# The low parts of the first projection's weights, and three products of the key blocks, on VectorE in place of GpSimd

## The chip, the cores and the metric

The kernel runs on one core of a Trainium2 chip. The metric is the device time of one execution in microseconds (us); the number to predict is the median of the runs of the changed kernel. The engines are TensorE (PE in the rows, its weight loads PEld), VectorE (DVE), ScalarE (ACT), GpSimd (POOL) and the queues of SyncE (SP), which issue the loads here.

## What is computed

A network of two blocks on 512 tokens of width 1024, all in float32. The first block is a hybrid mixer (a gated delta rule and a state space part, both in two directions) and an expert-choice feed-forward; the second has two layers of feed-forward, three kinds of attention and feed-forward. The change lies in the first mixer alone, whose beginning is

```python
proj = jnp.einsum('bld,dp->blp', n, w_in)                # 1024 -> 6720 columns
conv_in, gates, scal = jnp.split(proj, [CONV_CH, CONV_CH + GATE_CH], axis=-1)
c = jax.nn.silu(centred_dwconv(conv_in, conv_w, conv_b))  # 7 taps along the tokens
q, k, v, xs, Bm, Cm = jnp.split(c, [...], axis=-1)
...
kk = jnp.einsum('bnhid,bnhjd->bnhij', k, k)               # in gated_delta_chunked
A = jnp.where(strict, beta[..., :, None] * kk * decay, 0.0)
sol = lax.linalg.triangular_solve(A, rhs, left_side=True, lower=True, unit_diagonal=True)
```

## The kernel before

**Products in three.** A float32 product is made of three matmuls of a reduced float32 type: a weight tile of 1024 rows by 128 columns is loaded as `raw`, ScalarE copies its rounded high part to `whi` (L225), and another engine subtracts it to get the low part `wlo` (L226, in `weights`, called by `tiles`). `mm3` then runs high weights by high operands (L248), high by low (L249) and low by high (L250), eight times a tile. Each of `raw`, `whi` and `wlo` has two buffers in a ring, and `tiles` asks for a tile's weights one tile ahead. Which engine subtracts is an argument (`eng`); without one it is VectorE, as in the later feed-forwards.

**The projection.** `mix1_in` walks over 53 column tiles in a fixed order (`mix1_tiles`): keys, queries, values, inputs and states go through a convolution, gates do not. Tile i's low part is made by GpSimd up to the seventh tile from the end and by VectorE in the last six (L552). The first two tiles' weights are asked for earlier, while the input is turned, with GpSimd named there too (L2476). What follows a convolved tile: VectorE scales the product out of PSUM into `pad` (L603), ScalarE makes the first tap (L605), VectorE the other six (L609, two operands in SBUF), ScalarE the Silu (L615), and for values and inputs TensorE turns the result by token (L642). A gate is one VectorE operation (L671) and a Silu (L672). `mix_dve` and `step` spread these operations over the following tiles.

**The key blocks.** Once the keys are normed, `gdn_base` multiplies the keys of each chunk with themselves into a bank of PSUM, four heads at a time (L1105). ScalarE copies the bank to `KK` (L1107) and GpSimd takes the diagonal out in place (L1108), eight times. ScalarE copies the diagonal blocks together (L1115), VectorE transposes them (L1117), and for each direction GpSimd multiplies the decays by them (L1138) and VectorE by the step sizes (L1140). `gdn_forward` then does the substitution in 62 VectorE operations (L1154, L1157) between the taps, and four transposes (L1161, L1162).

**Order.** Every engine works through its instructions in a fixed order. A framework puts them in that order when the kernel is built, by places and priorities; an engine waits at the first one whose input is not there. Banks of PSUM: four for tiles' products, three for everything else, one for sums.

Of the kernel before, what the change touches and what calls it, by code (L numbers as in the profile page):

```python
# [25 lines left out]
def host_consts():  # L26
    """Tables that depend on the shapes alone."""
# [83 lines left out]
class Net:  # L111
# [14 lines left out]
    def psum_cfg(self, **bufs):  # L126
        """banks by use"""
        if self.ps_es is not None:
            self.ps_es.close()
        self.ps_es = ExitStack()  # L130
        self.ps = self.ps_es.enter_context(self.tc.tile_pool(name="psum", bufs=2, space=PSUM))
        self.ps_bufs = bufs

    def soon(self, n=300):
        """what frees a bank goes before other work of its engine"""
        return self.tc.high_priority(offset=n)

    def log_exp(self, done=None):
        """the tables with both functions, once the last activation of other ones is out"""
        with self.tc.issue_after(done.ins) if done is not None else ExitStack():  # L140
            self.nc.scalar.preload_act_table_set("natural_log_exp_and_others")
# [15 lines left out]
    def setup_first(self, p):  # L157
        """what the first operands need"""
# [47 lines left out]
    def ring(self, es, raw=2, hi=2, lo=2):  # L206
        """buffers of the weights on their way, for the whole network"""
# [9 lines left out]
    def weights(self, srcs, kt, cols, eng=None):  # L217
        """srcs: [(columns or None, dram ap [128, kt, n])]"""
# [10 lines left out]
    def tiles(self, reqs, eng=None, depth=1, then=None):  # L229
        """weights of each request (arguments of weights()) in turn, loaded ahead; then: requests of what comes next"""  # L230
# [28 lines left out]
    def sq_acc(self, pool, src, acc, first, tag="sq", bufs=2, last=False, scale=1.0, eng=None):  # L259
        """acc (+)= (src * scale)**2, or the last squares on their own"""  # L260
# [11 lines left out]
    def rstd_sum(self, pool, accs, n, tag="rstd", bufs=1, eps=EPS):  # L272
        """sum over partitions and accs / n + eps, by token"""
# [10 lines left out]
    def rstd_row(self, pool, v, tag="rstd", bufs=1):  # L284
        """v ** -0.5 by token, and as a row on every partition"""
# [22 lines left out]
    def rs(self):  # L308
        """inverse norms of the operands' tokens, made when first asked for"""
# [4 lines left out]
    def norm_open(self, side):  # L314
        """scratch of the preparation of the next operands, until norm_done()"""
# [3 lines left out]
    def norm_done(self):  # L319
# [5 lines left out]
        if self.accs2 is not None:  # L325
            # norm of a norm: (v * (w / v + eps)) ** -0.5, and the inner one for the residual
# [5 lines left out]
    def newton(self, pool, r, v, tag="nw"):  # L332
        """r <- r * (1.5 - 0.5 * v * r * r), r near v ** -0.5"""
# [6 lines left out]
    def split(self, hi, lo, src, scale=None, src2=None):  # L340
        """hi + lo == src * scale"""
# [10 lines left out]
class FFN:  # L352
# [9 lines left out]
    def prep(self, k, wv):  # L362
        """split xT[k] * wv into the operand pair and add its squares to the running sum"""
# [12 lines left out]
    def by_token(self, k, wv):  # L376
        """xT[k] * wv with the tokens on the partitions"""
# [11 lines left out]
    def prep2(self, k, w, wv):  # L389
        """prep() for operands that are normed twice, with w in between; the squares come in norm_done()"""  # L390
# [14 lines left out]
    def norm_residual(self, w):  # L405
        """the residual itself, after the first of two norms"""
# [4 lines left out]
    def load_x(self, p, wv=None, between=None):  # L411
        """the input with the features on the partitions, as operand pairs, or as the residual in two kinds of pieces"""
# [30 lines left out]
    def first_norm(self, p):  # L443
        """inverse norms of the input's tokens"""
# [62 lines left out]
# how far the delta rule is emitted before each of the last tiles of the projection  # L507
# [3 lines left out]
class Mix1:  # L511
# [1 line left out]
    def mix1_tiles(self):  # L513
        """column tiles of the projection in the order in which they are taken: (kind, tile)"""
# [21 lines left out]
    def step(self, n=1):  # L536
        """one more piece of everything that is under way"""
# [9 lines left out]
    def mix1_in(self, es_tab, es_qkv, then=None):  # L547
        """es_tab, es_qkv: what outlives the projection until the end of the mixer, of the delta rule"""
# [3 lines left out]
        W = self.tiles(self.mix1_reqs(), eng=lambda i: G if i < len(order) - 6 else V, then=then)  # L552
# [13 lines left out]
        # small weights  # L566
# [14 lines left out]
        # step biases and decay rates, the same on every partition  # L581
# [15 lines left out]
        # ---- what follows each kind of column tile  # L597
# [21 lines left out]
        def heads(n, f, ps):  # L619
            """queries or keys of a head, and their squares' sum by token"""  # L620
            if n == "q":
                # their norms come in with those of the output: see GDN.squares()
# [57 lines left out]
        for i, (n, f) in enumerate(order):  # L680
            n_[0] = i + 1
            if i >= len(order) - len(AHEAD):
                # what is left of the projection needs nothing but the operands: the delta rule begins meanwhile
# [32 lines left out]
    def mix_dve(self):  # L716
        """finish the taps of the oldest column tile, turn about with the next one's and the block inverses"""
# [13 lines left out]
    def sums(self, pn, h, sq):  # L731
        """sum of sq over the partitions, by token, into column h of each chunk"""
# [4 lines left out]
    def head_rows(self, p, pn, n, eps=EPS):  # L737
        """sums of squares of 8 heads by token -> (sum / n + eps) ** -0.5 in stacked rows"""
# [23 lines left out]
    def go(self, g):  # L762
        """under way, at twice the usual pace"""
        self.live.append(g)
        self.fast.append(g)

    def stack(self, pool, rows, n, tag):
        """rows [n, T] fp32 as exact hi (partitions 0..) and lo (partitions 64..) parts"""
# [8 lines left out]
    def bcast(self, ps, st, r, start=True, stop=True):  # L777
        """row r of a stack on every partition"""
        self.nc.tensor.matmul(ps, self.selr[:, r:r + 1].to_broadcast([128, 128]), st, start=start, stop=stop)

    def decays(self, wk, ps, sb):
        """step sizes and cumulated decays, by token and in rows"""
# [25 lines left out]
        # log1p(e) = 2 atanh(e / (2 + e))  # L808
# [24 lines left out]
        # rows: 16-23, 32-47 forward; 24-31, 48-63 backward  # L833
# [15 lines left out]
        # total decay of each chunk on every partition  # L849
# [18 lines left out]
# places in the order of emission: products of the delta rule's rows; start of the first group, and its early decays  # L868
# [5 lines left out]
class SSD:  # L874
    def wout_reqs(self, part):
        """weights of the output projection: of the delta rule's rows (0) or of the state space rows (1)"""
# [3 lines left out]
    def ssd_out(self, yp, wv, wg, before, after, then):  # L880
        """both directions of the state space part, gated and normed; x + mixed @ w_out; yp: pool of the operands"""
# [20 lines left out]
        # dt * decay to the end of the chunk; ln dt - cumulated decay  # L902
# [43 lines left out]
        def weigh(g, s, dd):  # L946
            """what the state takes in"""
# [4 lines left out]
        def inter(g, s, dd):  # L952
            """what the state gives out"""
# [20 lines left out]
        def decay(g, f, hh):  # L974
            """decays of one head in both directions, times the step sizes"""
# [106 lines left out]
# heads whose gate is GpSimd's  # L1082
# [3 lines left out]
class GDN:  # L1086
    def gdn_base(self):
        """products of the keys of a chunk, and the inverses of the 32 x 32 diagonal blocks, one block on each
        partition"""
# [10 lines left out]
        for c in range(4):  # L1100
            s = slice(c * 128, c * 128 + 128)
            for q in range(2):
# [3 lines left out]
                v = KK[:, c, 4 * q:4 * q + 4, :]  # L1106
                S_.copy(v, ps.rearrange("p (h i) -> p h i", h=4))  # L1107
                G.tensor_tensor(v, v, offd.unsqueeze(1).to_broadcast([128, 4, 128]), op=OP.mult)  # L1108
# [10 lines left out]
        for d in range(2):  # L1119
# [18 lines left out]
            G.tensor_tensor(e, e, kk, op=OP.mult)  # L1138
# [5 lines left out]
    def gdn_forward(self, b, Ab):  # L1144
        """forward substitution, an operation at a time"""
# [18 lines left out]
    def gdn_open(self):  # L1164
        """everything to be emitted for the delta rule in order"""
# [24 lines left out]
        def bc(col):  # L1190
            """[128, 4] of one scalar each head -> over the free dimension"""
# [11 lines left out]
        def unit(s, d, q, t):  # L1203
            """four heads of one chunk in one direction: (place in the order, what to emit)"""
# [8 lines left out]
            def rows():  # L1213
                # block inverses on the diagonal, rows of decays
# [42 lines left out]
            # (I + A)^-1 from its diagonal blocks  # L1257
# [30 lines left out]
            # the scan  # L1288
# [1268 lines left out]
```

## Time and profile before

| | us |
|---|---|
| three runs | 3308.85 (median), 3309.02, 3299.69 |
| span of the profiled execution | 3301.7 |
| granted TensorE clock, mean over the span | 0.977 |
| TensorE, VectorE, ScalarE, GpSimd busy | 3130.6, 1924.6, 1360.2, 716.8 |

The profiled execution's own time is not listed beside its span; the span is 7.2 us under the median of the three runs. A matmul's busy time overlaps with that of the next, so the share of TensorE is not what is left to win. The projection ends at about 415 us of the span; what follows is not touched.

### The profile page before, as it was taken

What the parts mean: (1) busy time and instruction counts of PE and PEld (TensorE: products, weight loads), DVE (VectorE), ACT (ScalarE), POOL (GpSimd) and SP (SyncE); (2) the same over time, 40 slices, a digit from 0 to 9 for tenths busy, and PEclk for the clock granted to TensorE, in tenths of its full rate; (3) what the DMA queues carried; (4) which work ended last, traced back from release to release, by engine and by line L of the source; (5) the groups of instructions that cost most, each with busy time, mean ns of one, the idle gap of its engine ahead of it and who ended that gap; (6) DMA issues with size and microseconds to landing.
All of it is one profiled execution on the core that took longest, in us unless ns stands there. A gap on an engine that the chain in (4) does not pass through costs nothing.

```text
span 3301.7 us, 39167 instructions
## 1 busy us (share of the span) xinstructions
PE 3130.6 (95%) x14939; PEld 2465.8 (75%) x14939; DVE 1924.6 (58%) x2762; ACT 1360.2 (41%) x2181; POOL 716.8 (22%) x509
## 2 busy tenths in 40 slices
PE   8988999799799899999999999999999999999998
PEld 6766799656576578888776788888888776688887
DVE  6889845644799874433768444334443577644432
ACT  5533443244677642222547333223232355632222
POOL 3453246441656610001220100010000222010000
PEclk9999999899899999999999999999999999999999
DMA  3322400314589823333230233333333331033332
GB/s 107 89 68 82 128 20 1 115 48 157 193 311 329 285 71 96 96 94 96 62 84 7 76 97 96 98 94 96 96 95 100 89 78 53 14 91 94 96 95 84
DMA packets 482536, 336.95 MB, mean 102 GB/s; under 512 B 36079, under 2 KB 428718, under 8 KB 482350
## 3 DMA queue, kind: packets, MB, share of 16 engines
q1 hardware_dynamic: 482350, 334.46, 33.5%
q8 instruction: 118, 1.93, 0.2%
q14 instruction: 68, 0.56, 0.1%
HBM read 324.45 MB, written 9.96 MB: 101 GB/s over the span
## 4 chain that ended last, share of the span: by engine, by line
PE 65%; DVE 5%; issue 3%; ACT 2%; POOL 2%; DMA 0%; DVEq 0%; POOLq 0%; ACTq 0%; SPq 0%
PE mm L248 17%; PE mm L250 17%; PE mm L249 17%; PE mm L1536 3%; PE pn L2258 2%; PE aux L2244 1%; PE aux L1646 1%; DVE sbe L2377 1%; PE mm L2299 1%; PE aux L278 1%; PE mm L2301 1%; POOL elo L1523 1%; POOL wlo L1523 1%; DVE elo L1523 1%; PE pn L1536 1%
## 5 line engine op out<-in xcount | busy, mean ns | idle before, releaser
L225 ACT CAST whi<-raw 128x1024 fp32r<-128x1024 f32 (+1 forms) x395 | 406.5, 1029 | 1181.3 <-PE mm L249 1045.9
L250 PE MATMUL mm<-xh,wlo 128*128 128x512 f32 (+1 forms) x2136 | 850.0, 398 | 19.1 <-POOL wlo L226 14.7
L248 PE MATMUL mm<-xh,whi 128*128 128x512 f32 (+1 forms) x2136 | 853.4, 400 | 3.7 <-DVE ckv L1849 2.8
L249 PE MATMUL mm<-xl,whi 128*128 128x512 f32 (+1 forms) x2136 | 848.9, 398 | 0.0
L226 DVE TENSOR_TENSOR wlo<-raw,whi 128x1024 fp32r<-128x1024 f32 (+1 forms) x342 | 411.8, 1204 | 297.6 <-ACT whi L225 288.3
L250 PEld LDWEIGHTS mm<-xh,wlo 128*128 128x128 f32 (+1 forms) x2136 | 406.4, 190 | 115.6 <-POOL wlo L226 18.6
L248 PEld LDWEIGHTS mm<-xh,whi 128*128 128x128 f32 (+1 forms) x2136 | 407.1, 191 | 96.3 <-issue 6.1
L249 PEld LDWEIGHTS mm<-xl,whi 128*128 128x128 f32 (+1 forms) x2136 | 406.5, 190 | 89.3
L269 POOL TENSOR_TENSOR acc<-acc,sq 128x512 f32<-128x512 f32 x46 | 77.9, 1694 | 1555.4 <-ACT sq L266 1251.2
L249 PE MATMUL mm<-hl,whi 128*128 128x512 f32 x704 | 274.6, 390 | 0.0
L248 PE MATMUL mm<-hh,whi 128*128 128x512 f32 x704 | 274.0, 389 | 0.0
L250 PE MATMUL mm<-hh,wlo 128*128 128x512 f32 x704 | 273.9, 389 | 0.0
L609 DVE SCALAR_TENSOR_TENSOR cacc<-pad,cw,cacc 128x512 f32<-128x512 f32 x216 | 221.0, 1030 | 13.6 <-ACT cacc L605 10.6
L481 DVE TENSOR_TENSOR u<-mm,rstd 128x512 f32<-128x512 f32 x88 | 60.8, 691 | 279.4 <-PE mm L250 279.4
L226 POOL TENSOR_TENSOR wlo<-raw,whi 128x1024 fp32r<-128x1024 f32 (+2 forms) x53 | 134.6, 2540 | 233.0 <-ACT whi L225 208.5
L477 DVE TENSOR_TENSOR g<-mm,rstd 128x512 f32<-128x512 f32 x88 | 60.8, 691 | 183.4 <-PE mm L250 182.2
L250 PEld LDWEIGHTS mm<-hh,wlo 128*128 128x128 f32 x704 | 132.2, 188 | 27.5
L248 PEld LDWEIGHTS mm<-hh,whi 128*128 128x128 f32 x704 | 132.1, 188 | 27.5
L249 PEld LDWEIGHTS mm<-hl,whi 128*128 128x128 f32 x704 | 132.2, 188 | 27.2
L1523 POOL TENSOR_TENSOR wlo<-eraw,whi 128x320 fp32r<-128x320 f32 x58 | 80.5, 1396 | 53.5 <-ACT whi L1521 46.4
L2204 ACT ACTIVATE Pt<-mm,smst 128x512 f32<-128x512 f32 (+3 forms) x144 | 75.4, 529 | 26.6 <-DVE smst L2203 21.6
L1523 POOL TENSOR_TENSOR elo<-eraw,ehi 128x320 fp32r<-128x320 f32 x57 | 77.5, 1369 | 36.7 <-ACT ehi L1521 29.4
(677 smaller groups left out, 5150.8 us busy)
## 6 DMA issues: line engine op xcount, KB each, us to landing
raw<-in_ffn_w_gate_dram SPq DMA_DIRECT2D x88, 512.0 KB
raw<-in_ffn_w_up_dram SPq DMA_DIRECT2D x88, 512.0 KB
raw<-in_w_in_dram SPq DMA_DIRECT2D x82, 512.0 KB
raw<-in_ffn_w_down_dram SPq DMA_DIRECT2D x64, 512.0 KB
eraw<-in_w_down_dram SPq DMA_DIRECT2D x52, 512.0 KB
eraw<-in_w_gate_dram SPq DMA_DIRECT2D x48, 512.0 KB
eraw<-in_w_up_dram SPq DMA_DIRECT2D x44, 512.0 KB
raw<-in_w_out_dram SPq DMA_DIRECT2D x32, 512.0 KB
```

The costliest lines, as they stand in the source:

```text
L225: nc.scalar.copy(hi, raw)
L226: (eng or nc.vector).tensor_tensor(lo, raw, hi.bitcast(F), op=OP.subtract)
L248: mm(ps, wh, xh, start=start, stop=False)
L249: mm(ps, wh, xl, start=False, stop=False)
L250: mm(ps, wl, xh, start=False, stop=stop)
L269: (eng or nc.gpsimd).tensor_tensor(acc, acc, s, op=OP.add)
L477: nc.vector.tensor_tensor(g, pg, self.rs, op=OP.mult)
L609: V.scalar_tensor_tensor(ac, pad[:, t:t + T], cw[:, i:i + 1], ac, op0=OP.mult, op1=OP.add)
L1523: eng.tensor_tensor(lo[:, c], raw[:, c], hi[:, c].bitcast(F), op=OP.subtract)
L1536: P.matmul(ps, x if n == 2 else x.bitcast(F), w[i][:, cols], start=first and i == 0, stop=last and i == n - 1)
L2204: S_.activation(h.Pt[:, QOFF[qc]:QOFF[qc] + n], ps[:, :n], AF.Exp, bias=st[:, 0, qc:qc + 1], accum_out=st[:, 1, qc:qc + 1])
L2258: P.matmul(po[64 * r:64 * r + 64, kc * 128:], h.v[:, kc], h.PT[:, o:o + 512 - kc * 128], start=start and kc == 0, stop=stop and kc == 3, s ...
```

## The change

Three edits, and the removal of comments and docstrings, which is left out here.

```diff
-        W = self.tiles(self.mix1_reqs(), eng=lambda i: G if i < len(order) - 6 else V, then=then)
+        W = self.tiles(self.mix1_reqs(), then=then)
...
-                v = KK[:, c, 4 * q:4 * q + 4, :]
-                S_.copy(v, ps.rearrange("p (h i) -> p h i", h=4))
-                G.tensor_tensor(v, v, offd.unsqueeze(1).to_broadcast([128, 4, 128]), op=OP.mult)
+                V.tensor_tensor(KK[:, c, 4 * q:4 * q + 4, :], ps.rearrange("p (h i) -> p h i", h=4),
+                                offd.unsqueeze(1).to_broadcast([128, 4, 128]), op=OP.mult)
...
-            G.tensor_tensor(e, e, kk, op=OP.mult)
+            V.tensor_tensor(e, e, kk, op=OP.mult)
```

The low parts of tiles 2 to 46 are made by VectorE. The diagonal of the key products is taken out by one VectorE operation that reads PSUM and writes `KK`, in place of a ScalarE copy and a GpSimd product. The decays' product with the key blocks is VectorE's, twice.

## Rows read from the trace of the kernel before

**Rows 1.** The page: VectorE's busy tenths in 40 slices of 82.5 us.
```profile
DVE  6889845644799874433768444334443577644432
```

**Rows 2.** Windows, five stages of the projection: length, busy us (instructions) by engine, clock, DMA.
```profile
41.25:95.00 53.75, 49.48 (x219) 39.90 (x220) 47.93 (x68) 26.42 (x37) 19.26 (x7) 0.90 0.28 77
95.00:206.00 111.00, 97.32 (x434) 78.44 (x434) 87.70 (x94) 51.40 (x64) 55.91 (x26) 0.92 0.27 78
206.00:309.00 103.00, 86.34 (x351) 67.33 (x349) 102.60 (x135) 31.81 (x43) 35.96 (x13) 0.93 0.27 75
309.00:371.00 62.00, 54.58 (x237) 43.71 (x238) 58.05 (x60) 21.97 (x32) 20.25 (x8) 0.94 0.35 103
371.00:415.00 44.00, 39.55 (x189) 32.56 (x188) 33.96 (x47) 20.84 (x30) 7.88 (x6) 0.92 0.47 140
```

**Rows 3.** VectorE's timeline: start, time from first start to last end, operation.
```profile
308.35 4.85 DVE L609 SCALAR_TENSOR_TENSOR cacc<-pad,cw,cacc 128x512 f32<-128x512 f32 x7
...
321.59 9.32 DVE L609 SCALAR_TENSOR_TENSOR cacc<-pad,cw,cacc 128x512 f32<-128x512 f32 x7
...
382.40 0.68 DVE L603 TENSOR_TENSOR pad<-mm,rstd 128x512 f32<-128x512 f32 x1
383.00 0.74 DVE L609 SCALAR_TENSOR_TENSOR cacc<-pad,cw,cacc 128x512 f32<-128x512 f32 x1
383.66 1.22 DVE L226 TENSOR_TENSOR wlo<-raw,whi 128x1024 fp32r<-128x1024 f32 x1
384.79 3.11 DVE L609 SCALAR_TENSOR_TENSOR cacc<-pad,cw,cacc 128x512 f32<-128x512 f32 x4
```

**Rows 4.** GpSimd's timeline beside those taps; in brackets the idle time before.
```profile
321.35 2.40 POOL L226 TENSOR_TENSOR wlo<-raw,whi 128x1024 fp32r<-128x1024 f32 x1 [4.64 <-ACT whi L225]
326.94 2.64 POOL L226 TENSOR_TENSOR wlo<-raw,whi 128x1024 fp32r<-128x1024 f32 x1 [3.19 <-ACT whi L225]
```

**Rows 5.** Windows of line 609 alone: length, VectorE busy us (instructions), clock, DMA.
```profile
41.25:95.00 53.75, 22.65 (x28) 0.90 0.28 77
95.00:206.00 111.00, 59.24 (x53) 0.92 0.27 78
206.00:309.00 103.00, 56.42 (x54) 0.93 0.27 75
309.00:371.00 62.00, 54.08 (x52) 0.94 0.35 103
371.00:415.00 44.00, 17.92 (x24) 0.92 0.47 140
```

**Rows 6.** VectorE's timeline: one operation beside a GpSimd split, and the next one alone.
```profile
62.13 2.62 DVE L818 SCALAR_TENSOR_TENSOR dt<-dt,e 128x256 f32<-128x256 f32 x1
...
65.34 0.41 DVE L818 SCALAR_TENSOR_TENSOR dt<-dt,e 128x256 f32<-128x256 f32 x1
```

**Rows 7.** Windows of line 226 alone: length, VectorE and GpSimd busy us (instructions), clock, DMA.
```profile
41.25:95.00 53.75, 0.00 (x0) 19.26 (x7) 0.90 0.28 77
95.00:206.00 111.00, 0.00 (x0) 35.66 (x14) 0.92 0.27 78
206.00:309.00 103.00, 0.00 (x0) 35.96 (x13) 0.93 0.27 75
309.00:371.00 62.00, 0.00 (x0) 20.25 (x8) 0.94 0.35 103
```

**Rows 8.** Groups by line, 0 to 420 us: busy us, mean ns, idle before and its releaser.
```profile
L1108 POOL TENSOR_TENSOR KK<-KK,offd 128x512 f32<-128x512 f32 x8 | 11.9, 1514 | 0.0
L1138 POOL TENSOR_TENSOR Ab<-Ab,kk 128x1024 f32<-128x1024 f32 x2 | 5.7, 2859 | 6.5 <-DVE kk L1117 6.5
```

**Rows 9.** Waits of TensorE, 41.25 to 371 us: total us, times, longest.
```profile
PE aux L642 <- ACT vt L615: 14.8, 4, 4.7
PE mm L250 <- POOL wlo L226: 14.7, 8, 4.5
```

**Rows 10.** TensorE's timeline: the wait at the first tile whose low part VectorE makes.
```profile
378.72 0.79 PE L250 MATMUL mm<-xh,wlo 128*128 128x512 f32 x1 [4.45 <-DVE wlo L226]
```

**Rows 11.** Groups by line, 0 to 420 us: an operation of VectorE on 1024 columns.
```profile
L1140 DVE TENSOR_TENSOR Ab<-Ab,bB 128x1024 f32<-128x1024 f32 x2 | 4.6, 2279 | 1.9 <-POOL Ab L1138 1.9
```

## The prediction

> **What bounds the kernel now.** The change touches one stage, so I first read where VectorE is loaded: its slices show 8 and 9 tenths from the second slice to the fifth [rows 1]. That is the input projection, which ends near 415 us (the later slices of 7 to 9 are the experts', which the change leaves alone). The windows of its stages [rows 2] show VectorE busy for 47.93 of 53.75 us, 87.70 of 111, then 102.60 of 103 and 58.05 of 62. From 206 to 371 us VectorE is simply full, and TensorE is paced by it. TensorE's own column there is no measure, as matmul times overlap; the waits are: before 371 us it stood 14.7 us for low parts from GpSimd and 14.8 us for Silu outputs that came late [rows 9]. Those outputs wait for the taps on VectorE. The clock column says the same: TensorE was granted 0.90 to 0.94 of full speed in every stage, because it had idled.
>
> The second question is what VectorE is full of. Two runs of seven taps, same shape, took 4.85 us at 308.35 and 9.32 us at 321.59 [rows 3]. Beside the second stood two splits of GpSimd, at 321.35 and 326.94 [rows 4]; beside the first none. So one split costs VectorE (9.32 - 4.85) / 2 = 2.2 us of standing still, though it runs on another engine. It is no matter of the tap: a 256-column operation takes 2.62 us beside a split and 0.41 alone [rows 6].
>
> **The change part by part.**
>
> *Splits.* 42 of the GpSimd splits between 41 and 371 us (7, 14, 13 and 8 by stage) go to VectorE [rows 7] (the other three moved ones lie before). What VectorE pays for one is seen at the end of the projection, where it makes them already: 383.66 to the next start at 384.79 is 1.13 us [rows 3]. 42 x 1.13 = 47.5 us are added.
>
> *Holds that go.* From 371 to 415 us, with no split on GpSimd, a tap is 17.92 / 24 = 0.747 us [rows 5]. By that, the taps of the four earlier stages are longer by 22.65 - 28 x 0.747 = 1.7, 59.24 - 53 x 0.747 = 19.6, 56.42 - 54 x 0.747 = 16.1 and 54.08 - 52 x 0.747 = 15.2 us, 52.7 in all. Other VectorE operations were held as well; I count ten in the timeline like the one of rows 6, at about 2.1 us each: four in the first stage (8.6), three in the second (6.4), three in the third (5.8). That makes 10.3, 26.0, 21.9 and 15.2, together 73 us. Bounds: 52.7 (taps alone) and 42 x 2.2 = 92 (every split holds something). The Trainium skill, "SBUF — State Buffer", section "Who interferes with whom", would go further than the count: it has a VectorE instruction with two SBUF inputs contend with a GpSimd instruction that reads SBUF, and the later one blocked until the first is done. By it a hold could last a whole split of 2.4 us, and 42 of them 101 us, 28 more than I count; the two splits of rows 4 held less than their length, so the count stands.
>
> *Mask.* Eight VectorE operations from PSUM, 512 columns, are added. The nearest row is the scaling out of PSUM, 382.40 to 383.00, so 0.60 us each [rows 3], 4.8 in all. Eight ScalarE copies go, which cost nothing there as ScalarE is under half busy [rows 2], and 11.9 us of GpSimd [rows 8]. The added wait: the mask waits for the key product, and the next taps and pads stand behind it; and TensorE, which needs a bank of the three, now waits for VectorE where it waited for ScalarE. I take nothing for that wait, since the ScalarE copies stood behind Silus that waited for the same taps; its bound is one wait of the longest kind in rows 9, 4.7 us.
>
> *Block products.* Two operations on 1024 columns, at the split's 1.13 to 1.22 us [rows 3]; the like of line 1140 has a mean of 2.279 only because the first of its two ran beside a GpSimd product [rows 11]. 2 x 1.2 = 2.4 us. Gone are two GpSimd products, mean 2.859 us, and the 6.5 us that GpSimd's queue stood before them for VectorE's transpose [rows 8], with the next low part queued behind: one of the eight waits of rows 9, the longest or next to it.
>
> *Queues.* The weight loads on SyncE's queue wait for a split to free `raw`; they now wait for VectorE's. The split stands behind the scaling of the tile two before it; that scaling waits for its tile's product, and TensorE has a whole tile to run meanwhile. So the new wait costs nothing while VectorE is within a tile of TensorE. What it costs otherwise is seen at 378.72: 4.45 us, when VectorE was behind [rows 10], and the clock of that stage is 0.92, or 0.08 x 44 = 3.5 us of full-speed work lost [rows 2].
>
> *Sum.* VectorE by stage: 41 to 95 us: -10.3 + 7.9 = -2.4. 95 to 206: -26.0 + 15.8 + 4.8 + 2.4 = -3.0. 206 to 309: -21.9 + 14.7 = -7.2. 309 to 371: -15.2 + 9.0 = -6.2. In time:
> - 41 to 95: VectorE is nearly full, TensorE waits in a chain on it: -3 (0 to -7, the latter with its clock loss of 0.10 x 53.75 = 5.4 back as well).
> - 95 to 206: not full, so its own 3.0 plus the wait behind the block product, 4, plus half of the clock loss of 0.08 x 111 = 8.9: -11 (+3, if the mask holds TensorE up, to -18).
> - 206 to 309: full throughout, so VectorE's sum is the time: -7 (-2, with the low bound of holds, to -13).
> - 309 to 371: by the sum -6; by the parts, a tile is 0.60 + 6 x 0.66 + 1.13 = 5.7 us on VectorE [rows 3], 8 tiles 46, which is -16 with TensorE no slower. I take -10, between them.
> - 371 to 415: the 4.45 us wait comes from VectorE's backlog; half of it goes: -2 (0 to -7).
>
> Together -33 us; the ends, which won't all meet, are about -5 and -60. What follows 415 us is the same instructions, started earlier; nothing in it is timed from the start, so I carry the gain through whole. The span is 3301.7; with the same 7.2 us around it the forecast is 3308.85 - 33 = 3276 us.
>
> **The rivals.**
> 1. *TensorE becomes the bound* and its waits on VectorE go: the two rows of waits, 29.5 us [rows 9], and of the clock loss of the first four stages, 5.4 + 8.9 + 0.07 x 103 + 0.06 x 62 = 25 us [rows 2], some 20, as the rest falls into the waits: -50, 3259. For it: a tile of 5.7 us on VectorE, by parts. Against it: the substitution's operations keep 206 to 309 us full.
> 2. *Only the full stages gain*, -7 - 6 = -13, 3296, because the chains of 41 to 206 us (decays, key norms, key blocks) have their own length. The 14.8 us for Silus speak for it.
> 3. *Given back*: the mask and the chain take back what the full stages gain, 3309, within what can be told apart.
> 4. *Lockstep, slower.* Low parts now come from the engine that is full, and TensorE loses the lead that GpSimd's splits let it have. The mechanism has been seen once, at 378.72 [rows 10]; with the clock that is 4.45 + 3.5 = 8 us a time. If it strikes where VectorE has more work than TensorE, every other one of the 13 tiles from 206 to 309 us and two at the key blocks, eight times in all, it is 64 - 33 = +31, 3340. It decides from about four such waits beyond those that go. Against it: one tile of lead remains, and where VectorE is the bound a TensorE wait costs nothing of its own.
> 5. *The split was rightly GpSimd's.* If the long taps have another cause than the splits, no hold goes, and 47.5 + 4.8 + 2.4 = 55 us are added to a full engine: 3364. The two runs of taps and the pair of equal operations speak against it [rows 3, 4, 6]. The Trainium skill, "Perfetto Trace Analysis", section "Optimizing Scalar/DVE Operations", has a rule on this side: offloading from a saturated VectorE, even to GpSimd, may make sense; it adds that the port they share may defeat it, which is what the trace shows here, at 2.2 us a split.
>
> **How the numbers follow.** Forecast 0.50, rival 1 0.13, rival 2 0.15, rival 3 0.09, rival 4 0.09, rival 5 0.04. A difference under 0.3% (10 us) can't be told from none here. Faster holds the forecast and rivals 1 and 2, 0.78; same 0.09; slower 0.13. The range takes the forecast with most of its bounds and rivals 1 and 2, and stops short of the slower ones: 3250 to 3302.
>
> **What would show it.** Right: no tap over 0.8 us from 41 to 371 us but beside the two affine selects that stay on GpSimd; line 226 on VectorE at 1.22 us, about 51 times by 415 us; the windows of 206 to 371 us shorter, by some 17 us together; the wait of line 250 for low parts, now from VectorE, under 14.7 us; the granted clock of these stages above 0.94. Wrong: taps still at 2.8 us (rival 5); many waits of 4 us of line 250 for VectorE and a lower clock (rival 4); key products waiting for `KK` on VectorE by more than 5 us (rival 3).

## The result, and where the time went

| | before | after |
|---|---|---|
| median of the runs shown, us | 3304.8 (3299.7 to 3309.0) | 3257.5 (3256.5 to 3260.9) |
| span of the profiled execution, us | 3301.7 | 3254.8 |
| mean granted clock of TensorE | 0.977 | 0.982 |

The changed kernel takes 0.9861 of the time, with a 95% interval of 0.9847 to 0.9875: 47 us less, where 33 were forecast. The direction and the range held; the size was short by 14 us.

VectorE's busy tenths, which answer to [rows 1], first: the fuller slices now end at the fourth, and the projection's last tile, which began at 416 us, begins at 370.

```profile
DVE  6899654554999854435777444334443577644432
```

Fixed windows, as in [rows 2], shift against the work when the work gets shorter. So I cut both traces at three places that can be recognised in VectorE's timeline: the first operation of the blocks' substitution (207.0 us before, 185.7 after), the end of its last transposes (306.1 and 267.6), and the start of the projection's last tile on TensorE (415.8 and 370.3). The columns are the window and its length, the busy times of PE, PEld, DVE, ACT and POOL with their instructions, the granted clock, the DMA share and GB/s. Before:

```profile
28.00:207.00 179.00, 160.75 (x713) 128.04 (x712) 148.64 (x173) 83.46 (x106) 80.84 (x35) 0.92 0.28 78
207.00:306.10 99.10, 82.75 (x337) 64.78 (x336) 98.72 (x129) 30.17 (x40) 35.96 (x13) 0.93 0.27 77
306.10:415.80 109.70, 97.51 (x443) 78.77 (x442) 95.30 (x110) 45.16 (x65) 28.13 (x14) 0.94 0.39 116
```

After:

```profile
28.00:185.70 157.70, 154.02 (x721) 123.63 (x720) 140.29 (x210) 80.34 (x99) 2.98 (x2) 0.98 0.32 92
185.70:267.60 81.90, 70.10 (x285) 52.01 (x283) 81.90 (x132) 27.01 (x36) 0.00 (x0) 0.96 0.26 74
267.60:370.30 102.70, 100.83 (x476) 83.03 (x477) 89.85 (x123) 46.77 (x66) 7.97 (x6) 0.98 0.44 134
```

The three lengths fall by 21.3, 17.2 and 7.0 us, 45.5 in all; the rest of the kernel passes that through, as the span is 46.9 us shorter. Splitting each length into VectorE's busy time and the remainder gives the next table (length, less the DVE column, is VectorE's idle time):

| stretch | forecast: busy, idle, sum | measured: busy, idle, sum |
|---|---|---|
| to the substitution | -5.4, -8.6, -14 | -8.4, -13.0, -21.3 |
| substitution | -7.2, +0.2, -7 | -16.8, -0.4, -17.2 |
| to the last tile | -6.2, -5.8, -12 | -5.4, -1.6, -7.0 |
| sum | -18.8, -14.2, -33 | -30.6, -14.9, -45.5 |

In the second stretch VectorE is busy for all of 81.90 us and nothing else matters. In the first and the third VectorE has idle time, and TensorE sets the pace: it is busy for 154.02 of 157.70 and 100.83 of 102.70 us there, at 0.98 of its clock, and all its waits there sum to 3.4 and 3.2 us, where they were 18.2 and 12.2 before. (Busy times of matmuls overlap, so the small waits say more than the 98%.)

The groups of the first 420 us show the two sides of the exchange (busy us, mean ns of one, idle before and its releaser). The taps answer to [rows 3] and [rows 5], the splits to [rows 7], the block product and its follower to [rows 8] and [rows 11]:

```profile
L609 DVE SCALAR_TENSOR_TENSOR cacc<-pad,cw,cacc 128x512 f32<-128x512 f32 x216 | 157.6, 745 | 2.1 <-ACT cacc L605 0.6
L226 DVE TENSOR_TENSOR wlo<-raw,whi 128x1024 fp32r<-128x1024 f32 (+1 forms) x53 | 65.2, 1230 | 3.0 <-ACT whi L225 3.0
L1106 DVE TENSOR_TENSOR KK<-aux,offd 128x512 f32<-128x512 f32 x8 | 5.3, 682 | 0.0
L1139 DVE TENSOR_TENSOR Ab<-Ab,bB 128x1024 f32<-128x1024 f32 x2 | 2.4, 1223 | 0.0
L1137 DVE TENSOR_TENSOR Ab<-Ab,kk 128x1024 f32<-128x1024 f32 x2 | 2.4, 1204 | 0.0
```

The same taps before:

```profile
L609 DVE SCALAR_TENSOR_TENSOR cacc<-pad,cw,cacc 128x512 f32<-128x512 f32 x216 | 221.0, 1030 | 13.6 <-ACT cacc L605 10.6
```

So 216 unchanged operations got 63.4 us shorter, 1030 to 745 ns each, because another engine stopped working beside them. VectorE's 44 additional splits after 28 us cost 44 x 1.13 = 50 us of its time; the 45th, of 512 columns, lies before. The product with line 1139, the old line 1140, fell from 2279 to 1223 ns though nothing in it was changed.

TensorE's waits between 41 and 371 us of the new kernel answer to [rows 9] (total us, times, longest):

```profile
PE mm L250 <- DVE wlo L226: 10.5, 10, 3.2
PE mm L248 <- ACT whi L225: 5.0, 7, 0.9
PE aux L642 <- ACT vt L615: 1.3, 2, 1.1
```

The waits for Silu outputs went from 14.8 to 1.3 us. Those for low parts went from 14.7 to 10.5 us, from an engine that is now full, and the longest of them is 3.2 us where [rows 10] had 4.45.

### The profile page after: what moved, and what is told of

It is laid out like the page before. It is cut to its first block, busy times and chain, and to the rows that moved or that the text cites. A ratio compares the mean times of both kernels' runs of the same rounds, so it can differ in the third digit from the quotient of the medians.

```text
span 3254.8 us, 39119 instructions
## 1 busy us (share of the span) xinstructions
PE 3114.5 (96%) x14939; PEld 2452.0 (75%) x14939; DVE 1894.1 (58%) x2817; ACT 1355.6 (42%) x2172; POOL 582.9 (18%) x454
## 4 chain that ended last, share of the span: by engine, by line
PE 66%; DVE 5%; issue 3%; POOL 2%; ACT 2%; DMA 0%; POOLq 0%; DVEq 0%; ACTq 0%; SPq 0%
PE mm L248 18%; PE mm L249 18%; PE mm L250 18%; PE mm L1535 3%; PE pn L2257 2%; PE aux L2243 1%; PE aux L1645 1%; DVE sbe L2376 1%; POOL wlo L1522 1%; PE mm L2298 1%; PE mm L2300 1%; PE aux L278 1%; POOL elo L1522 1%; DVE elo L1522 1%; PE aux L2061 0%
## 5 line engine op out<-in xcount | busy, mean ns | idle before, releaser
L225 ACT CAST whi<-raw 128x1024 fp32r<-128x1024 f32 (+1 forms) x395 | 406.9, 1030 | 1249.3 <-PE mm L249 1093.6
L250 PE MATMUL mm<-xh,wlo 128*128 128x512 f32 (+1 forms) x2136 | 844.4, 396 | 10.5 <-DVE wlo L226 10.5
L226 DVE TENSOR_TENSOR wlo<-raw,whi 128x1024 fp32r<-128x1024 f32 (+2 forms) x387 | 466.4, 1205 | 300.0 <-ACT whi L225 290.6
L609 DVE SCALAR_TENSOR_TENSOR cacc<-pad,cw,cacc 128x512 f32<-128x512 f32 x216 | 157.6, 745 | 2.1 <-ACT cacc L605 0.6
L2202 DVE TENSOR_REDUCE smst<-mm 128x1 f32<-128x512 f32 (+3 forms) x144 | 68.8, 481 | 27.0 <-PE mm L2300 14.3
```

The lines of the kernel that those rows point to most:

```text
L225: nc.scalar.copy(hi, raw)
L226: (eng or nc.vector).tensor_tensor(lo, raw, hi.bitcast(F), op=OP.subtract)
L250: mm(ps, wl, xh, start=False, stop=stop)
L609: V.scalar_tensor_tensor(ac, pad[:, t:t + T], cw[:, i:i + 1], ac, op0=OP.mult, op1=OP.add)
L2202: V.tensor_reduce(st[:, 0, qc:qc + 1], ps[:, :n], axis=AX.X, op=OP.max, negate=True)
```

## The experiments

All ten kernels are edits of the changed kernel: two undo one part of the change each, four add work to it, and four go further in its direction. Times are medians; each ratio is to the kernel before in the same session, with its 95% interval.

### The splits alone, and the rest alone

The first is the changed kernel with the mask and the block products put back where they were:

```diff
-                V.tensor_tensor(KK[:, c, 4 * q:4 * q + 4, :], ps.rearrange("p (h i) -> p h i", h=4),
-                                offd.unsqueeze(1).to_broadcast([128, 4, 128]), op=OP.mult)
+                v = KK[:, c, 4 * q:4 * q + 4, :]
+                S_.copy(v, ps.rearrange("p (h i) -> p h i", h=4))
+                G.tensor_tensor(v, v, offd.unsqueeze(1).to_broadcast([128, 4, 128]), op=OP.mult)
...
-            V.tensor_tensor(e, e, kk, op=OP.mult)
+            G.tensor_tensor(e, e, kk, op=OP.mult)
```

> The changed kernel with the mask and the two block products put back on ScalarE and GpSimd, so that of the change only the 45 splits are left. If the holds of VectorE beside GpSimd's splits were the cost (theory 1), most of the gain stays: 3268 us (3260 to 3280), the mean tap near 0.77 us, with some taps at 1.7 beside the GpSimd masks. If the gain came from the chain through the key blocks (theory 2: GpSimd's queue stood behind them), it falls back to 3290 or more.

Measured: 3264.9 us, ratio 0.9882 (0.9866 to 0.9899), 38 us less than before. The second is the opposite, the mask and the products on VectorE and the splits still on GpSimd:

```diff
-        W = self.tiles(self.mix1_reqs(), then=then)
+        W = self.tiles(self.mix1_reqs(), eng=lambda i: G if i < len(order) - 6 else V, then=then)
```

> The kernel before with the mask and the two block products on VectorE; the 45 splits stay on GpSimd. Theory 1: the taps stay long (mean 1.0 us) and little is won, 3293 us (3285 to 3302). Theory 2: most of the gain is here, 3270 us or less. If the two parts add up, the gains of this run and of the one with the splits alone sum to 47 us.

Measured: 3295.6 us, ratio 0.9979 (0.9968 to 0.9989), 7 us less. The two parts add up: 38 + 7 = 45 of 47 us. The taps say which part took the holds away. With the splits alone on VectorE:

```profile
L609 DVE SCALAR_TENSOR_TENSOR cacc<-pad,cw,cacc 128x512 f32<-128x512 f32 x216 | 163.5, 773 | 2.2 <-ACT cacc L605 0.6
```

and with the mask and products alone:

```profile
L609 DVE SCALAR_TENSOR_TENSOR cacc<-pad,cw,cacc 128x512 f32<-128x512 f32 x216 | 214.1, 998 | 11.6 <-ACT cacc L605 8.8
```

1030, 998, 773 and 745 ns for none, the rest, the splits and all: nearly all of the holds were the splits', but the mask and the products on GpSimd held VectorE too, 163.5 - 157.6 = 6 us of taps. The other pair has 221.0 - 214.1 = 7 us, but that is no net gain: the substitution's operations, 37.9 us before (lines 1154 and 1157), take 42.0 in the kernel with mask and products alone, held by the splits that stay. One hold by a block product, in the kernel with the splits alone, on VectorE's and GpSimd's timelines (start, time, operation):

```profile
171.60 3.05 DVE L226 TENSOR_TENSOR wlo<-raw,whi 128x1024 fp32r<-128x1024 f32 x1
174.58 2.85 DVE L609 SCALAR_TENSOR_TENSOR cacc<-pad,cw,cacc 128x512 f32<-128x512 f32 x1
171.19 5.69 POOL L1138 TENSOR_TENSOR Ab<-Ab,kk 128x1024 f32<-128x1024 f32 x2 [6.48 <-DVE kk L1117]
```

A split that takes 1.22 us alone and a tap that takes 0.75 last from 0.41 us after the start of GpSimd's two block products to 0.55 us after their end. The profile books this standing still as busy time of VectorE, not as idle time.

### Is it the company of GpSimd, or its reading?

If the long taps came from the splits themselves, GpSimd work that nobody needs must bring them back. This kernel is the changed one with one more GpSimd product over two SBUF operands for each of the 45 moved splits (44 of them of 1024 columns); its output goes to a scratch tile:

```diff
+        if x:
+            j = self.junk[:, :kt * cols].rearrange("p (k c) -> p k c", k=kt)
+            nc.gpsimd.tensor_tensor(j, hi.bitcast(F), hi.bitcast(F), op=OP.mult)
```

> The changed kernel, and for each of the 45 tiles one GpSimd product of the high part with itself, 1024 columns, read from SBUF, into scratch that nobody reads. Nothing waits for it but the reuse of the scratch and of the high part's buffer. Theory 1: VectorE is held by some 2 us a tile again, now on top of its own splits: mean tap 1.0 us or more, 3320 us (3300 to 3345). Theory 2, or any theory in which the time of GpSimd's split mattered and not its company: 3258 us, within 5.

Measured: 3312.5 us, ratio 1.0030 (1.0018 to 1.0042). 55 us more than the changed kernel, for work that no other instruction needs; in its trace no engine waits for that product either. The groups and one place of the timelines:

```profile
L614 DVE SCALAR_TENSOR_TENSOR cacc<-pad,cw,cacc 128x512 f32<-128x512 f32 x216 | 198.4, 933 | 2.5 <-ACT cacc L610 1.1
L230 POOL TENSOR_TENSOR junk<-whi 128x1024 f32<-128x1024 f32 x44 | 102.2, 2323 | 243.6 <-ACT whi L225 243.6
```

```profile
226.28 0.51 DVE L1158 TENSOR_TENSOR tmp<-Ab,Tb 128x350 f32<-128x350 f32 x1
226.72 0.68 DVE L608 TENSOR_TENSOR pad<-mm,rstd 128x512 f32<-128x512 f32 x1
227.32 1.61 DVE L1161 TENSOR_TENSOR Tb<-Tb,tmp 128x350 f32<-128x350 f32 x1
226.33 2.21 POOL L230 TENSOR_TENSOR junk<-whi 128x1024 f32<-128x1024 f32 x1 [9.36 <-ACT whi L225]
```

The scaling `pad`, one of whose inputs is in PSUM, runs in its usual 0.68 us in the middle of GpSimd's product (the 36 scalings have a mean of 681 ns in this run and of 685 in the changed kernel). The next operation, with both inputs in SBUF and 0.51 us long alone, starts at 227.32 and ends when GpSimd does: 226.33 + 2.21 = 228.54, and 0.39 later. So a hold lasts from the first such operation of VectorE to the end of GpSimd's, which is why the 2.2 us of the forecast is a little less than a split's 2.4. The ends agree over the whole run: of the 30 taps over 0.85 us, 29 end 0.54 or 0.55 us after the end of such a product. That is the rule of the Trainium skill, "SBUF — State Buffer", section "Who interferes with whom", for a VectorE instruction with two SBUF inputs beside a GpSimd instruction that reads SBUF; here the two agree. Not only operations with two SBUF inputs were held, though. In the kernel before, a copy of 32 columns with one took 2.33 us beside a split that ran from 101.09 to 103.87 us; in the changed kernel it takes 0.17:

```profile
101.57 2.33 DVE L1123 COPY cols<-Ct 128x32 f32<-128x32 f32 x1
```

Next, the same with fills, which only write SBUF, two of 1024 columns a tile behind a product of one column:

```diff
+        if x:
+            nc.gpsimd.tensor_tensor(self.junk[:, :1], hi[:, 0, :1].bitcast(F), hi[:, 0, :1].bitcast(F), op=OP.mult)
+            nc.gpsimd.memset(self.junk, 0.0)
+            nc.gpsimd.memset(self.junk, 0.0)
```

> As the run with the extra GpSimd product, but the extra work only writes SBUF: two zero fills of 1024 columns a tile, some 2 us, after a product of one column that waits for the high part. If the hold is of reads (theory 1): taps stay at 0.75 us and the time at 3258 us (3254 to 3266). If any GpSimd work beside VectorE holds it (theory 3): as with the extra product, 3300 us or more.

Measured: 3257.0 us, ratio 0.9866 (0.9850 to 0.9883), the same as the changed kernel.

```profile
L615 DVE SCALAR_TENSOR_TENSOR cacc<-pad,cw,cacc 128x512 f32<-128x512 f32 x216 | 157.8, 746 | 3.0 <-ACT cacc L611 1.5
```

```profile
303.17 1.22 DVE L227 TENSOR_TENSOR wlo<-raw,whi 128x1024 fp32r<-128x1024 f32 x1
304.30 3.52 DVE L615 SCALAR_TENSOR_TENSOR cacc<-pad,cw,cacc 128x512 f32<-128x512 f32 x5
302.90 0.39 POOL L229 TENSOR_TENSOR junk<-whi 128x1 f32<-128x1 f32 x1 [3.58 <-ACT whi L225]
303.36 0.96 POOL L230 MEMSET junk<- 128x1024 f32 x1
304.37 0.95 POOL L231 MEMSET junk<- 128x1024 f32 x1
```

The taps have the mean of the changed kernel. The split takes its usual 1.22 us beside the first fill, and the taps that follow 0.70 each, the first of them beside the second fill. So it is GpSimd's reading, here of two operands, that holds the taps. Two small operations with one input were longer beside a fill and ended with it: a copy of 32 columns (1.03 us for 0.17) and a scaling of 4 (0.73 for 0.17). The third kernel has one SBUF input in place of two:

```diff
+            nc.gpsimd.tensor_scalar(j, hi.bitcast(F), 2.0, None, op0=OP.mult)
```

> As the run with the extra GpSimd product (3312 us), but the extra operation has one input: the high part of 1024 columns times 2, read from SBUF, into scratch. If a GpSimd operation holds VectorE for as long as it reads, this one holds it for its own, shorter time: taps between 0.8 and 0.95 us in the mean, 3285 us (3268 to 3305). If only a GpSimd operation with two inputs holds VectorE: 3257 us, within 6.

Measured: 3273.7 us, ratio 0.9910 (0.9890 to 0.9931): 16 us more than the changed kernel, between the two others.

```profile
L614 DVE SCALAR_TENSOR_TENSOR cacc<-pad,cw,cacc 128x512 f32<-128x512 f32 x216 | 173.2, 817 | 2.5 <-ACT cacc L610 1.1
L230 POOL TENSOR_SCALAR junk<-whi 128x1024 f32<-128x1024 f32 x44 | 138.4, 3145 | 171.3 <-ACT whi L225 171.3
```

```profile
246.14 3.13 POOL L230 TENSOR_SCALAR junk<-whi 128x1024 f32<-128x1024 f32 x1 [7.16 <-ACT whi L225]
246.56 1.52 DVE L614 SCALAR_TENSOR_TENSOR cacc<-pad,cw,cacc 128x512 f32<-128x512 f32 x1
248.00 0.61 DVE L1161 TENSOR_TENSOR Tb<-Tb,tmp 128x440 f32<-128x440 f32 x1
```

One tap is 0.78 us longer, the next operation is not, though GpSimd's is recorded until 249.27. The tap ends 1.19 us before that, and so it is in the whole run: of the 27 taps over 0.85 us, 26 end 1.19 or 1.20 us before the one-input operation does, whether that takes 2.8 or 4.5 us, where they ended 0.55 us after the two-input one. So the hold ends a fixed time before the recorded end. The recorded ends of GpSimd are rough, and no run shows how long it reads; what makes the hold so short stays open.

### What a microsecond of VectorE is worth

Each moved split is made twice:

```diff
         nc.vector.tensor_tensor(lo, raw, hi.bitcast(F), op=OP.subtract)
+        if x:
+            nc.vector.tensor_tensor(lo, raw, hi.bitcast(F), op=OP.subtract)
```

> The changed kernel with each of the 45 moved splits made twice on VectorE, which adds 45 x 1.13 = 51 us of work to it and no work of GpSimd. If VectorE still bounds the stage from the key blocks to the end of the substitution and is near the bound elsewhere: 3290 us (3278 to 3305). If TensorE bounds most of the projection now and VectorE has the room: 3265 us or less.

Measured: 3297.6 us, ratio 0.9990 (0.9978 to 1.0001), 40 us more than the changed kernel, for 44 x 1.13 = 50 us of additional VectorE work. Four fifths of it end in the time. The three stretches, cut at the same places, show where:

```profile
28.00:200.70 172.70, 160.24 (x715) 125.59 (x714) 164.53 (x234) 82.37 (x101) 2.98 (x2) 0.95 0.29 84
200.70:295.30 94.60, 76.77 (x289) 57.15 (x287) 92.16 (x141) 26.25 (x35) 0.00 (x0) 0.89 0.23 64
295.30:410.30 115.00, 105.59 (x482) 85.00 (x483) 101.54 (x136) 48.80 (x68) 7.32 (x6) 0.96 0.41 120
```

They are 15.0, 12.7 and 12.3 us longer, for 23, 10 and 11 doubled splits, or 26, 11 and 12 us. In the substitution, where VectorE was full, all of the work ends in the time. In the first stretch 11 us of it went into VectorE's idle time. In the third VectorE had been idle for 12.9 us, and yet all of the work ends in the time. Work that is added can make VectorE the limit where it was not, so this run does not show that VectorE bounds the first and third stretch of the changed kernel; it shows how little room is left there. TensorE's waits of 41 to 420 us show how it gets through:

```profile
PE mm L253 <- DVE wlo L229: 18.3, 12, 3.3
```

Twelve waits, none over 3.3 us. Even with twice the splits on the full engine the low parts are not later than by that; the lockstep of rival 4, with waits of 4 us and more, does not appear.

### Going on in the same direction

The two first splits, which were left on GpSimd, also to VectorE:

```diff
-        self.load_x(self.norm_p, self.w1, lambda: self.ahead.append(self.weights(*next(first), eng=nc.gpsimd)))
+        self.load_x(self.norm_p, self.w1, lambda: self.ahead.append(self.weights(*next(first))))
```

> The changed kernel with the first two tiles' splits on VectorE too. They stand while the input is turned, VectorE idle between its operand splits. 2.4 us become 1.2 us twice, and if TensorE waits for them there: 3256 us (3252 to 3260); a hold by GpSimd plays no part. If VectorE's wait for ScalarE's copy stands before an operand split: 3262.

Measured: 3255.3 us, ratio 0.9861 (0.9839 to 0.9883), 2 us less than the changed kernel and within what can be told apart. The same, with the 1.76 us zero fill of `Tb` before the substitution given to GpSimd in exchange, since fills held no taps:

```diff
-        V.memset(Tb, 0.0)
+        self.nc.gpsimd.memset(Tb, 0.0)
```

> The changed kernel with the first two tiles' splits on VectorE and the 1.76 us zero fill before the substitution moved from VectorE to GpSimd, where it only writes. 2 us for the splits, as measured with them alone, and 1.8 us for the fill, as VectorE is full there: 3254 us (3250 to 3257). If a fill on GpSimd holds VectorE after all, 3256 us.

Measured: 3257.0 us, ratio 0.9856 (0.9837 to 0.9876). No difference can be seen from either. Then the experts' splits, of which GpSimd makes 320 of 1024 columns, all to VectorE:

```diff
-                for eng, c in ((G, slice(0, self.GW)), (V, slice(self.GW, 1024))) if i > 4 else ((G, slice(0, 1024)),):
+                for eng, c in ((V, slice(0, 1024)),):
```

> The changed kernel with GpSimd's share of the experts' splits (320 of 1024 columns, some 150 pieces) on VectorE as well. There a VectorE operation of 704 columns has a mean of 1.06 us beside GpSimd's 1.4. If the holds are most of that and the stage is bound by the engines, 1.13 us for all 1024 columns: 3245 us (3235 to 3255). If the loads bound that stage (0.9 of the DMA engines' time): 3258 us, within 6. If VectorE, 0.9 busy there, becomes the bound: 3270 or more.

Measured: 3259.4 us, ratio 0.9864 (0.9839 to 0.9889), no change. The window of the changed kernel in that stage, with the columns as above:

```profile
940.00:1020.00 80.00, 77.79 (x333) 54.15 (x332) 77.15 (x97) 59.71 (x78) 50.03 (x39) 1.00 0.93 333
```

VectorE is nearly full there, with GpSimd busy for 50 us beside it, and yet nothing is gained. One reason is in the groups of 780 to 1160 us, the changed kernel first:

```profile
L1522 DVE TENSOR_TENSOR wlo<-eraw,whi 128x704 fp32r<-128x704 f32 x58 | 61.1, 1058 | 5.4 <-ACT whi L1520 3.7 <-PE mm L1535 1.0 <-DMA raw<-in_w_down_dram 0.3
L1522 DVE TENSOR_TENSOR wlo<-eraw,whi 128x1024 fp32r<-128x1024 f32 x58 | 70.0, 1219 | 1.3 <-ACT whi L1520 0.7
```

A piece costs VectorE 1.06 us with GpSimd's help and 1.22 without. In that time VectorE is busy for 325.75 us in the one kernel and 336.31 in the other, so the move did not relieve it at all, whatever holds went. In the window the DMA engines are busy for 0.93 of the time and TensorE for 77.79 of its 80 us, at full clock; which of the three is the limit there, this run does not show. Last, the 46 additions of squares of line 269, from GpSimd to VectorE:

```diff
-        (eng or nc.gpsimd).tensor_tensor(acc, acc, s, op=OP.add)
+        (eng or nc.vector).tensor_tensor(acc, acc, s, op=OP.add)
```

> The changed kernel with the 46 additions of squares (512 columns, mean 1.70 us on GpSimd) on VectorE at 0.7 us. They lie at the ends of the stages, where four of them stand in the chain that ended last after the experts, 1.6 us each. Expected 3252 us (3245 to 3258), won at those ends only; if VectorE's other work there is pushed back, 3262.

Measured: 3262.6 us, ratio 0.9882 (0.9859 to 0.9904). No gain, if anything 5 us more, with overlapping intervals, though the operation itself got shorter. In the changed kernel:

```profile
L269 POOL TENSOR_TENSOR acc<-acc,sq 128x512 f32<-128x512 f32 x46 | 78.2, 1699 | 1556.2 <-ACT sq L266 1250.5 <-DVE wlo L226 305.4
```

and here, where six that VectorE made already stand in the same row:

```profile
L269 DVE TENSOR_TENSOR acc<-acc,sq 128x512 f32<-128x512 f32 x52 | 36.9, 726 | 7.4 <-ACT sq L266 7.4
```

The 3252 us expected were missed, and the 3262 for VectorE's other work being pushed back met. That this is the cause was not shown: VectorE is idle for a quarter to a half of the windows in which these additions lie (37.11 busy of 50 us from 1110, 28.89 of 60 from 740), and no run separates a hold from a wait there.

## Why the forecast held, and why it was short

**What held: the mechanism.** A GpSimd split holds VectorE for longer than VectorE needs to make it. The kernel with added GpSimd reads and the one with added fills show it from both sides, and rivals 4 and 5 fall: no lockstep appeared (waits of at most 3.2 us), and the splits were not rightly GpSimd's. Rival 2 falls as well, since the stretch that was not full gained most, 21.3 us, and rival 3 with it. What was said to show it: one tap alone is over 0.8 us, 0.89 beside an affine select, as was excepted, and their mean is 0.745; line 226 made 51 splits on VectorE after 28 us; line 250's waits are 10.5 where under 14.7 was said; the clock is 0.96 to 0.98; and of the key products' wait for `KK` on VectorE, which was to stay under 5 us, no row is left among TensorE's (in the kernel with mask and products alone it is 2.6 us, once). The stretch from 206 to 371 us, said to become 17 us shorter, did so by 17.2 + 7.0 = 24 together with the tiles behind it, for which 2 more were forecast.

**What failed: the size of the holds.** The table of the three stretches says where the missing us are: VectorE's busy time fell by 30.6 us where 18.8 were forecast, its idle time by 14.9 where 14.2 were. The term that was too small is the 73 us of holds, with ends at 52.7 and 92. By the groups of the three stretches it came out at 84: the ten other operations held 21.1 us, as counted, but the taps 221.0 - 157.6 = 63.4, where 52.7 were taken. Three causes make up nearly all of these 10.7 us. Ten taps between 28 and 41 us, ahead of the windows of [rows 5], took 10.69 us, 3.4 too long. A tap among many takes 157.6 / 216 = 0.730 us, not 0.747, which is 3 us in 187. And a tap that the edge of a window cuts stands in both windows of [rows 5]: together with the ten they hold 221 taps where there are 216, so five too many, 3.7 us, were taken for work that stays.

**The splits and the rest.** Without the terms for the mask (+4.8), the products (+2.4) and the wait that they were to remove (-4), the forecast is -33 - 3 = -36 us, and the kernel with the splits alone measured -38. That they agree is luck. The 73 us are all long operations of VectorE, whatever GpSimd did beside them, so what masks and block products held is in them too ([rows 11] has such a hold, one of the ten). In the kernel with the splits alone it stays: its taps are 5.9 us longer than those of the changed kernel, and one split takes 3.05 us for 1.22. With these 8 us booked to the mask and the products, the forecast for the splits alone is some -28, short by 10, and for the rest -5, where done alone it measured -7.

In the substitution the forecast was 21.9 us of holds less 14.7 for 13 splits. The holds of that stretch, from the groups of both traces, were 22.7: the taps 54.7 us for 51 against 34.2 for 46, which is 16.8 beyond the five missing ones, and lines 1154 and 1157 5.9 us. That was right; but only ten splits and 46 taps fell into the shorter stretch, 18 rather than 15 splits into the next, and two scalings of 0.68 us fewer. I had priced the stage with its old load of tiles, though a stage that gets shorter holds fewer of them. What left it came back behind it, where the forecast was -12 and the measurement -7.0.

**What comes after VectorE: rival 1.** The forecast built every stage on VectorE's sum, and added waits and clock to it. In the substitution VectorE's sum was the time. In the first and third stretch of the changed kernel TensorE hardly waits any more, as rival 1 had it, and its time of 3259 us is nearer to the measured one than the forecast's. By its own terms: the waits of TensorE in the three stretches sum to 46.7 us before and 16.9 after, 30 less where the rival had 29.5, and its clock loss, worked out from the clock column as in the prediction, to 28 and 8, 19 less where it had some 20. Part of that is luck, as the two rows of [rows 9] kept 11.8 of their 29.5 us and other waits went in their place, and in the substitution VectorE is full and TensorE waits 10.3 us. The two readings don't exclude each other: what went are VectorE's holds, and what is left to TensorE once they are gone sets the time of two stretches of three.

**The mask and the block products.** The cost of the eight masks was right (682 ns each as recorded, against 0.68 for the scaling out of PSUM that they were priced by), and so was that of the two products (1204 ns for 1.2 us). The wait was sized by one TensorE wait, where a chain hung on it. The kernel before, on VectorE's, ScalarE's, TensorE's and again VectorE's timelines (start, time from first start to last end, operation, in brackets the idle time before and its releaser):

```profile
156.23 9.33 DVE L609 SCALAR_TENSOR_TENSOR cacc<-pad,cw,cacc 128x512 f32<-128x512 f32 x7
...
165.60 0.63 ACT L615 ACTIVATE qf<-cacc 128x512 f32<-128x512 f32 x1 [5.93 <-DVE cacc L609]
...
167.60 1.54 ACT L1107 COPY KK<-aux 128x512 f32<-128x512 f32 x3
...
168.22 1.16 PE L1105 MATMUL aux<-kf 128*128 128x128 f32 x8 [3.35 <-ACT KK L1107]
...
170.30 0.63 PE L248 MATMUL mm<-xh,whi 128*128 128x512 f32 x1
...
173.33 0.40 PE L250 MATMUL mm<-xh,wlo 128*128 128x512 f32 x1
...
176.55 0.69 DVE L603 TENSOR_TENSOR pad<-mm,rstd 128x512 f32<-128x512 f32 x1 [10.38 <-PE mm L250]
```

Seven taps take 9.33 us where 4.85 would do, beside a split and two masks on GpSimd. A Silu waits 5.93 us for the last of them, the copies of `KK` stand behind it on ScalarE, and TensorE's key products stop for 3.35 us for a bank that these copies free. The next column tile starts behind the key products, at the lower level of TensorE's clock (its matmuls are recorded at 0.63 us, later at 0.40). So VectorE, held at first, then stands idle for 10.38 us until that tile is done. The same scaling, the fourteenth, with the splits alone, with the mask and products alone, and in the changed kernel:

```profile
159.07 0.69 DVE L603 TENSOR_TENSOR pad<-mm,rstd 128x512 f32<-128x512 f32 x1 [4.13 <-PE mm L250]
171.53 0.69 DVE L603 TENSOR_TENSOR pad<-mm,rstd 128x512 f32<-128x512 f32 x1 [6.36 <-PE mm L250]
157.97 0.69 DVE L603 TENSOR_TENSOR pad<-mm,rstd 128x512 f32<-128x512 f32 x1 [2.97 <-PE mm L250]
```

So the chain has two links, and either change loosens it: with the splits moved the taps are done sooner, and the wait falls by 6.25 us though the copies still stand behind Silus; with the mask on VectorE the copies are gone, and it falls by 4.0. The whole stretch says the same. Up to the substitution VectorE was busy for 148.64 and idle for 30.4 us before. With mask and products alone (substitution from 200.6 us) it is busy for 151.88 and idle for 20.7: +3.2 where I had +7.2, and -9.6 where I had -4. With the splits alone (from 190.0 us) it is busy for 141.69 and idle for 20.3, -10.1. Both together take 13.0 off the idle time, not 19.7: in good part they remove the same waits. The prediction had seen the copies behind the Silus, and used it only to put the added wait at nothing; that TensorE, and behind it VectorE, wait for them was left out. That the idle time came out right in sum is luck as well, -13.0 for -8.6 before the substitution against -1.6 for -5.8 behind it.

The last us lie between the sum of the parts, 45, and the whole, 47, which the intervals don't separate.

## What to carry to other kernels

Where VectorE is full, price a GpSimd operation on two SBUF operands twice, once at GpSimd's duration and once at VectorE's loss: here up to 2.2 us of holding against 1.13 us to make the split itself. Look for it as two durations of one operation of the same shape on VectorE, not as idle time; here the scalings out of PSUM were free of it, and the taps beside GpSimd's fills. Sum the long operations over one window, since the edges of several count an operation twice. Then ask what sets the time once VectorE is relieved, and whether the move relieves it: the same move gave 38 us in the projection and nothing in the experts' stage, where VectorE has more to do without GpSimd's 320 columns than it lost beside them.

## What the chip showed that I had not expected

A one-input GpSimd operation on 1024 columns holds VectorE only briefly, 0.78 us of a tap, and is itself recorded as longer than the two-input one, 3145 against 2323 ns beside the same load; 45 of them cost 16 us where the two-input ones cost 55. And fills by GpSimd, 90 of them at 0.96 us, cost nothing that shows in the time, though VectorE was full in the substitution. The Trainium skill, "SBUF — State Buffer", section "Who interferes with whom", makes the difference between reading and writing for a VectorE instruction with two SBUF inputs, and the taps beside fills agree with it; the brief hold of the one-input read is not what it would lead to, since it makes no difference between one input and two of GpSimd's, and the run decides.
